# Latent attention's query projection: rotary columns taken once, and rotated for four heads together on VectorE

## The chip, the cores and the metric

One core of one Trainium2 chip runs the whole program. The time is device microseconds of one execution; the median of the runs is what is compared. In the text PE is TensorE (PEld its weight loads), DVE is VectorE, ACT is ScalarE, POOL is GpSimd and SP is the engine that issues the DMAs.

## What is computed

Two decoder layers on 256 tokens of width 1024, in float32. Each layer has parallel attention groups (eight heads of latent attention, eight heads of sparse attention), an output projection, cross-attention and a gated FFN. The change lies in the query side of the latent attention:

```python
def apply_rope(x, cos, sin):
    x1, x2 = jnp.split(x, 2, axis=-1)
    ...
    return jnp.concatenate([x1 * c - x2 * s, x1 * s + x2 * c], axis=-1)

def mla_mixer(cq, ckv, kr, cq_g, w_uq, ckv_g, w_ukv, cos, sin):
    q = (rms_norm(cq, cq_g) @ w_uq).reshape(B, S, MLA_HEADS, MLA_NOPE + MLA_ROPE)   # 8 heads x (64 + 32)
    kv = (rms_norm(ckv, ckv_g) @ w_ukv).reshape(B, S, MLA_HEADS, MLA_NOPE + MLA_V)
    q_nope = q[..., :MLA_NOPE]
    q_rope = apply_rope(q[..., MLA_NOPE:], cos, sin)
    k_nope, v = kv[..., :MLA_NOPE], kv[..., MLA_NOPE:]
    k_rope = apply_rope(kr[:, :, None, :], cos, sin)[:, :, 0]
    ...
        s = (jnp.einsum('bqhd,bkhd->bhqk', qn, k_nope)
             + jnp.einsum('bqhd,bkd->bhqk', qr, k_rope)).astype(jnp.float32) * scale
```

## The kernel before, in words

A float32 product is made of three matmuls on numbers split in two: `hi` is the rounded value and `lo` the rest, and hi x hi, lo x hi and hi x lo are added in PSUM. A piece of a weight is loaded by DMA into a `raw` buffer (four of them), ACT writes `hi` (L130), DVE writes `lo` = raw - hi (L131); `hi` and `lo` have six buffers each. The raw buffer is free for the next DMA when both have read it; a DMA that waits for one holds the queue of weights behind it, the pieces of the output projection `w_out` among them.

The attention of a layer is a list of steps, written in an order that is given for each layer (`mq0` to `mq3` are the calls of `mla_q` for two heads each, `mqk0` to `mqk3` those of `mla_qk`, `mkv` is `mla_kv`, `av` belongs to the sparse heads; the lists begin with the sparse heads' steps):

```
layer 0: ... ch qk3 kr mq2 mq0 fill mkv par2 mq1 mq3 av3 mqk2 mqk3 mqk0 mqk1 mav0 mav1 fill mav3 mav2
layer 1: ... ch qk3 kr mq0 mkv mq3 mq1 av3 mqk0 mq2 mqk1 mqk3 mav0 mav3 mqk2 mav1 mav2
```

A scheduler then orders the instructions of each engine by these steps, their dependences and its priorities. Each engine runs its list strictly in order. A PSUM tile is one bank: four for the tag `a` and four for the tag `b`; `mla` has `a`, the scores `mqk` have `b` in layer 0 and `a` in layer 1.

`mla_q` for two heads (`hp`) writes 256 columns of queries, 128 a head: 64 without rotation (nope), 32 for rotation, and these 32 once more with their halves swapped, made by two more splits of 128x96. Three tiles of the rank by three matmuls by two heads are 18 matmuls of 128x256 (L177 to L179). One DVE multiplication (L713) by a table with ones, cosines and sines moves both heads into `qT`. The scores (L721, L722) contract over 128 rows; on the key's side the rotated 32 rows stand twice, so the sum of the two products is the rotation. What follows for a head is a maximum on DVE (L545), an exponential on ACT (L548), a reciprocal and a product with it on DVE (L550, L154), transposes on PE (`pt`, L561) and their copy (`pT`, L564 on ACT or L566 on DVE; tag `pT`, four buffers), and the product with the values (`mpv`).

Of the kernel before, what the change touches and what calls it, by code (L numbers as in the profile page):

```python
# [10 lines left out]
F32 = mybir.dt.float32  # L11
# [42 lines left out]
def consts():  # L54
    f = np.float32
    ident = np.eye(P, dtype=f)
    q = np.arange(P)[:, None]
    k = np.arange(S)[None, :]
    dist = (P + q - k).astype(f)
    neg = np.where(dist >= 0, -dist, -BIG).astype(f)  # L60
    tri = np.where(dist >= 0, 0.0, -BIG).astype(f)
    inv = (np.float32(10000.0) ** (-np.arange(0, ROPE, 2, dtype=f) / np.float32(ROPE))).astype(f)
    ang = np.arange(S, dtype=f)[:, None] * inv[None, :]
    cos, sin = np.cos(ang).astype(f), np.sin(ang).astype(f)
    cs = np.ones((P, S), f)
    cs[64:80], cs[80:96] = cos.T, cos.T
    cs[96:112], cs[112:128] = -sin.T, sin.T
    kcs = np.concatenate([cos, cos, -sin, sin], 1).reshape(NT, P, 64).transpose(1, 0, 2)
    slopes = (2.0 ** (-8.0 * np.arange(1, HN + 1) / HN)).astype(f)
    t = np.arange(S).reshape(NT, P).T[:, :, None, None]  # L70
    cend = (np.arange(16) * 16 + 31)[None, None, None, :]
    ok = (cend <= t) & (np.arange(16) < NC)
    ok = np.broadcast_to(ok, (P, NT, HN, 16))
    ctab = np.where(ok, -(slopes * 8.0)[None, None, :, None] * (t - cend), -BIG).astype(f)
    return {
        "c_ident": ident, "c_neg": neg, "c_tri": tri, "c_cs": cs, "c_kcs": np.ascontiguousarray(kcs),
        "c_ctab": np.ascontiguousarray(ctab), "c_cok": np.ascontiguousarray(ok.astype(f)),
    }

# [10 lines left out]
def trunk(ctx: ExitStack, tc: tile.TileContext, a: dict, out: bass.AP):  # L90
# [41 lines left out]
        return hv, lv  # L132

    def wmat(w, cuts, ks=KD, cols=None, wn=None):
        """Column ranges of w [ks*128, :] split into (hi, lo), as a list over the rows' tiles."""
        n = sum(c1 - c0 for c0, c1 in cuts)
        per = max(1, 1024 // (wn or n))
        out_ = []
        for k0 in range(0, ks, per):
            k1 = min(ks, k0 + per)  # L140
            segs, o = [], 0
            for c0, c1 in cuts:
                segs.append(((0, k1 - k0), (o, o + c1 - c0),
                             w[k0 * P:k1 * P, c0:c1].rearrange("(k p) n -> p k n", p=P)))
                o += c1 - c0
            h, lo = piece(k1 - k0, n, segs, wn, cols)
            out_ += [(h[:, i], lo[:, i]) for i in range(k1 - k0)]
        return out_
# [15 lines left out]
        V.tensor_tensor(hl[1], x, hl[0].bitcast(F32), op=ALU.subtract)  # L164

    def mm_nat(o, xh_, xl_, t, ws):
        """o[token, col] += x @ w, x^T stationary."""
        for k, (h, lo) in enumerate(ws):
            T.matmul(o, xh_[:, t, k], h, start=k == 0, stop=False)  # L169
            T.matmul(o, xh_[:, t, k], lo, start=False, stop=False)  # L170
            T.matmul(o, xl_[:, t, k], h, start=False, stop=k == len(ws) - 1)  # L171

    def mm_tr(o, xh_, xl_, ws, m0):
        """o[col, token] += (x @ w)^T, w stationary."""
        ms = slice(m0, m0 + P)
        for k, (h, lo) in enumerate(ws):
            T.matmul(o, h[:, ms], xh_[:, :, k], start=k == 0, stop=False)  # L177
# [100 lines left out]
        return par[:, c:c + n]  # L278

    tri = const.tile([P, S], F32, name="c_tri", tag="c_tri")  # L280
    cs = const.tile([P, S], F32, name="c_cs", tag="c_cs")
    kcs = const.tile([P, NT, 64], F32, name="c_kcs", tag="c_kcs")
    ctab = const.tile([P, NT, HN, 16], F32, name="c_ctab", tag="c_ctab")
    cok = const.tile([P, NT, HN, 16], F32, name="c_cok", tag="c_cok")
# [79 lines left out]
    for l in range(DEPTH):  # L364
# [168 lines left out]
            V.tensor_tensor(ol[:, :, kt:kt + n], src, hi.bitcast(F32), op=ALU.subtract)  # L533

        def probs(heads, scale, shape, mult):
            """exp(scale * score + table - max) for each head; its rows' scales are left for norm()."""
            sm = st.tile(shape, F32, name="sm", tag="sm", bufs=8)
            out_ = []
            for parts, tables, sc, kind in heads:
# [150 lines left out]
        def mla_rope_k():  # L690
# [8 lines left out]
            else:  # L699
                for g in range(2):  # L700
                    V.tensor_copy(kT[g][64:128], pb[64:128, None, 0:S].to_broadcast([64, 4, S]))

        def mla_q(ch, hp):
            r2 = lambda v: v.rearrange("p k (h c) -> p (k h) c", h=2)
            cols = [(lambda v: r2(v), lambda v: r2(v)[:, :, 0:96]),
                    (lambda v: r2(v)[:, :, 80:96], lambda v: r2(v)[:, :, 96:112]),
                    (lambda v: r2(v)[:, :, 64:80], lambda v: r2(v)[:, :, 112:128])]
            ws = wmat(a["mla_w_uq"][l], [(hp * 192, (hp + 1) * 192)], ks=3, cols=cols, wn=256)
            pb = bank("mla")
            for i in range(2):  # L710
                mm_tr(pb[:, i * S:(i + 1) * S], ch[0], ch[1], ws, i * P)
            j = 2 * (hp % 2)
            V.tensor_tensor(qT[hp // 2][:, j:j + 2, :], pb.rearrange("p (i n) -> p i n", i=2),  # L713
                            cs[:, None, :].to_broadcast([P, 2, S]), op=ALU.mult)

        def mla_qk(hp):
            heads = []
# [61 lines left out]
        for name in cfg['attn'].split():  # L779
# [3 lines left out]
            if name in ("kr", "mq0", "mkv") and "qT" not in e:  # L783
                qT = e["qT"] = [big.tile([P, 4, S], F32, name=f"qT{g}", tag=f"q{g}") for g in range(2)]
                kT = [big.tile([P, 4, S], F32, name=f"kT{g}", tag=f"k{g}") for g in range(2)]
            steps[name]()

        gb = load_gb(a["ln1_g"][l], a["ln1_b"][l])
# [224 lines left out]
```

## Time and profile before

| | |
|---|---|
| median of three runs | 887.38 us (887.13, 887.38, 888.57) |
| profiled execution, span | 887.0 us |
| PE / PEld busy | 97% / 90% |
| DVE / ACT / POOL busy | 74% / 58% / 5% |
| chain that ended last | PE 88%, DVE 5%, DMA 3%, ACT 2% |

The profile is of one execution; its span stands 0.4 us under the median of the runs. Matmuls are pipelined, so the busy time of PE counts one matmul while the next has begun. The chain is followed back from the last instruction through what released each.

### The profile page before, as it was taken

The page shows a single profiled execution, that of the slowest core. Times are in us where ns is not written, and L with a number is a line of the kernel's source. Part 1 is how long each engine was busy: PE and PEld are TensorE (multiplying, and loading weights), DVE is VectorE, ACT ScalarE, POOL GpSimd, SP SyncE. Part 2 cuts the span into 40 slices and gives each one's busy share as a digit, 9 for nine tenths or more (in the row PEclk, how much of TensorE's full clock was granted, in tenths as well). Part 3 has the DMA queues.
Part 4 walks back from the last instruction along what each step waited for, and adds up shares of the span by engine and source line. Part 5 has one row for each costly group of instructions (what it writes and reads, how often), then busy time and mean ns, then how long its engine had stood idle before and what let it go on. Part 6 is the DMA issues. An engine that isn't in the chain of part 4 may idle for free.

```text
span 887.0 us, 15857 instructions
## 1 busy us (share of the span) xinstructions
PE 857.6 (97%) x6088; PEld 794.2 (90%) x6088; DVE 659.9 (74%) x1293; ACT 511.7 (58%) x938; POOL 44.8 (5%) x60
## 2 busy tenths in 40 slices
PE   3999999999999999999999999999999999999996
PEld 3989798899989999999989998879998899999995
DVE  6788887766587777677687788868566877767767
ACT  4669764545545565465555678636573476555551
POOL 1053100000000000000000020000000000000000
PEclk9999999999999999999999999999999999999998
DMA  8954463485247656556537734546633746656631
GB/s 243 301 154 122 130 188 99 144 260 166 95 143 238 190 178 208 184 167 206 176 119 199 216 90 109 143 131 212 192 116 110 236 149 205 200 161 188 214 122 48
DMA packets 128523, 149.76 MB, mean 169 GB/s; under 512 B 6289, under 2 KB 111039, under 8 KB 128447
## 3 DMA queue, kind: packets, MB, share of 16 engines
q1 hardware_dynamic: 128447, 148.75, 54.6%
q8 instruction: 48, 0.79, 0.4%
q14 instruction: 28, 0.23, 0.1%
HBM read 147.68 MB, written 1.05 MB: 168 GB/s over the span
## 4 chain that ended last, share of the span: by engine, by line
PE 88%; DVE 5%; DMA 3%; ACT 2%; issue 1%; SPq 0%; POOL 0%; DVEq 0%; ACTq 0%; POOLq 0%
PE up L179 9%; PE up L178 9%; PE up L177 9%; PE acc L947 4%; PE acc L948 4%; PE acc L949 4%; PE acc L170 3%; PE acc L169 3%; PE acc L171 3%; PE fill L171 2%; PE xq L179 2%; PE xq L178 2%; PE xq L177 2%; PE fill L169 2%; PE fill L170 2%; PE pt L561 2%
## 5 line engine op out<-in xcount | busy, mean ns | idle before, releaser
L131 DVE TENSOR_TENSOR lo<-raw,hi 128x1024 fp32r<-128x1024 f32 (+5 forms) x296 | 320.6, 1096 | 82.9 <-ACT hi L130 78.3
L130 ACT ACTIVATE hi<-raw 128x1024 fp32r<-128x1024 f32 (+5 forms) x296 | 279.7, 957 | 152.7 <-PE acc L171 34.6
L179 PE MATMUL up<-xTh,lo 128*128 128x256 f32 x672 | 190.2, 283 | 0.0
L178 PE MATMUL up<-xTl,hi 128*128 128x256 f32 x672 | 190.2, 283 | 0.0
L177 PE MATMUL up<-xTh,hi 128*128 128x256 f32 x672 | 190.2, 283 | 0.0
L178 PEld LDWEIGHTS up<-xTl,hi 128*128 128x128 f32 x672 | 128.9, 192 | 0.7
L177 PEld LDWEIGHTS up<-xTh,hi 128*128 128x128 f32 x672 | 128.9, 192 | 0.7
L179 PEld LDWEIGHTS up<-xTh,lo 128*128 128x128 f32 x672 | 128.9, 192 | 0.0
L931 DVE SCALAR_TENSOR_TENSOR cv<-up,par,cv 128x255 f32<-128x255 f32 x88 | 42.1, 479 | 51.6 <-ACT cv L930 51.5
L930 ACT ACTIVATE cv<-up,par 128x256 f32<-128x256 f32 x88 | 49.0, 559 | 52.6 <-PE up L179 48.0
L948 PE MATMUL acc<-lo,frh 128*128 128x512 f32 x176 | 68.8, 391 | 0.0
L947 PE MATMUL acc<-hi,frh 128*128 128x512 f32 x176 | 68.7, 392 | 0.0
L949 PE MATMUL acc<-hi,frl 128*128 128x512 f32 x176 | 68.2, 389 | 0.0
L548 ACT ACTIVATE p<-p,nm 128x128 f32<-128x128 f32 (+1 forms) x96 | 42.8, 450 | 9.5 <-DVE nm L545 9.3
L199 POOL TENSOR_TENSOR mv<-mv,mhalf 128x1 f32<-128x1 f32 x16 | 14.7, 920 | 650.5 <-DVE mv L223 497.6
L932 DVE SCALAR_TENSOR_TENSOR cv<-up,par,cv 128x254 f32<-128x254 f32 x88 | 42.0, 479 | 1.4
L937 ACT ACTIVATE frh<-cv 128x256 fp32r<-128x256 f32 x44 | 18.3, 419 | 37.8 <-DVE cv L935 37.6
L949 PEld LDWEIGHTS acc<-hi,frl 128*128 128x128 f32 x176 | 33.0, 188 | 7.5 <-DVE frl L938 0.6
L947 PEld LDWEIGHTS acc<-hi,frh 128*128 128x128 f32 x176 | 33.1, 188 | 6.9 <-ACT frh L937 0.8
L177 PE MATMUL projt<-xTh,hi 128*128 128x256 f32 x128 | 37.2, 292 | 1.9 <-DVE c2l L462 1.6
L948 PEld LDWEIGHTS acc<-lo,frh 128*128 128x128 f32 x176 | 33.1, 188 | 6.0
L178 PE MATMUL projt<-xTl,hi 128*128 128x256 f32 x128 | 37.0, 289 | 0.5 <-DVE xTl L240 0.5
(257 smaller groups left out, 2027.6 us busy)
## 6 DMA issues: line engine op xcount, KB each, us to landing
raw<-in_ffn_w_up SPq DMA_DIRECT2D x88, 512.0 KB, 4.9
raw<-in_ffn_w_down SPq DMA_DIRECT2D x44, 512.0 KB, 4.3
raw<-in_xa_wkv SPq DMA_DIRECT2D x32, 512.0 KB, 4.3
raw<-in_xa_wq SPq DMA_DIRECT2D x16, 512.0 KB, 4.6
raw<-in_xa_wo SPq DMA_DIRECT2D x16, 512.0 KB, 4.1
raw<-in_w_in SPq DMA_DIRECT2D x24, 256.0 KB, 4.8
raw<-in_w_out SPq DMA_DIRECT2D x16, 256.0 KB, 5.4
raw<-in_w_out SPq DMA_DIRECT2D x8, 512.0 KB, 5.1
```

Of the source, the lines that this page charges most:

```text
L130: A.activation(h_, x_, AF.Copy)
L131: V.tensor_tensor(l_, x_, h_.bitcast(F32), op=ALU.subtract)
L169: T.matmul(o, xh_[:, t, k], h, start=k == 0, stop=False)
L170: T.matmul(o, xh_[:, t, k], lo, start=False, stop=False)
L171: T.matmul(o, xl_[:, t, k], h, start=False, stop=k == len(ws) - 1)
L177: T.matmul(o, h[:, ms], xh_[:, :, k], start=k == 0, stop=False)
L178: T.matmul(o, h[:, ms], xl_[:, :, k], start=False, stop=False)
L179: T.matmul(o, lo[:, ms], xh_[:, :, k], start=False, stop=k == len(ws) - 1)
L930: A.activation(c, u, AF.Identity, bias=pcol("cb", l, ft), scale=w_[2])
L947: T.matmul(o, fh[:, ts_], h[:, cs_], start=f == 0, stop=False)
L948: T.matmul(o, fh[:, ts_], lo[:, cs_], start=False, stop=False)
L949: T.matmul(o, fl[:, ts_], h[:, cs_], start=False, stop=f == NF - 1)
```

## The change: rotary columns once, four heads at a time

`mla_q` now splits the 64 nope columns of its two heads (128x384 in all) and their 32 rotary columns (128x192) apart. The rotary columns of two calls (a pair: hp 0 and 1, or 2 and 3) go into one pair of tiles, `rhi` and `rlo`, from the same buffers as `hi` and `lo`, held until the second call of the pair. Each call has nine matmuls for nope; the second call of a pair has nine more for the rotary rows of four heads, into the other half of its PSUM bank. So a pair has 27 matmuls instead of 36. ACT copies the nope rows of each head into `qT`. In the second call of a pair DVE rotates 128 rows: a shuffle that swaps the halves of each head's 32 rows, a product with the cosines, one with the sines, and a sum; then four copies of 32x256, two on DVE and two on ACT, put the heads' rows into rows 64 to 95 of `qT`. Rows 96 to 127 are set to zero by GpSimd once a layer. `rc` and `rs` are two buffers of the tag `pT`.

```diff
-    cs = const.tile([P, S], F32, name="c_cs", tag="c_cs")
+    cs = const.tile([P, 2, S], F32, name="c_cs", tag="c_cs")
...
+        rw = {}
+
         def mla_q(ch, hp):
-            r2 = lambda v: v.rearrange("p k (h c) -> p (k h) c", h=2)
-            cols = [(lambda v: r2(v), lambda v: r2(v)[:, :, 0:96]),
-                    (lambda v: r2(v)[:, :, 80:96], lambda v: r2(v)[:, :, 96:112]),
-                    (lambda v: r2(v)[:, :, 64:80], lambda v: r2(v)[:, :, 112:128])]
-            ws = wmat(a["mla_w_uq"][l], [(hp * 192, (hp + 1) * 192)], ks=3, cols=cols, wn=256)
+
+            g, i = divmod(hp, 2)
+            last = g in rw
+            if not last:
+                rw[g] = [wp.tile([P, 3, P], F32R, name="r" + s, tag=s, bufs=HL) for s in ("hi", "lo")]
+            rh, rl = rw[g]
+            r = wp.tile([P, 1024], F32, name="raw", tag="raw", bufs=RAW)
+            rv = r[:, :576].rearrange("p (k n) -> p k n", k=3)
+            nc.sync.dma_start(rv, a["mla_w_uq"][l][:, hp * 192:(hp + 1) * 192].rearrange("(k p) n -> p k n", p=P))
+            h, lo = [wp.tile([P, 3, P], F32R, name=s, tag=s, bufs=HL) for s in ("hi", "lo")]
+            heads = lambda v: v.rearrange("p k (h c) -> p k h c", h=2)
+            ms = slice(64 * i, 64 * i + 64)
+            for cut, dh, dl in ((slice(0, 64), h, lo), (slice(64, 96), rh[:, :, ms], rl[:, :, ms])):
+                src, dh, dl = heads(rv)[:, :, :, cut], heads(dh), heads(dl)
+                A.activation(dh, src, AF.Copy)
+                V.tensor_tensor(dl, src, dh.bitcast(F32), op=ALU.subtract)
             pb = bank("mla")
-            for i in range(2):
-                mm_tr(pb[:, i * S:(i + 1) * S], ch[0], ch[1], ws, i * P)
-            j = 2 * (hp % 2)
-            V.tensor_tensor(qT[hp // 2][:, j:j + 2, :], pb.rearrange("p (i n) -> p i n", i=2),
-                            cs[:, None, :].to_broadcast([P, 2, S]), op=ALU.mult)
+            mm_tr(pb[:, 0:S], ch[0], ch[1], [(h[:, k], lo[:, k]) for k in range(3)], 0)
+            if last:
+                mm_tr(pb[:, S:2 * S], ch[0], ch[1], [(rh[:, k], rl[:, k]) for k in range(3)], 0)
+            for j in range(2):
+                A.activation(qT[g][0:64, 2 * i + j, :], pb[64 * j:64 * j + 64, 0:S], AF.Copy)
+            if last:
+                del rw[g]
+                rc, rs = [tmp.tile([P, S], F32, name=n, tag="pT", bufs=4) for n in ("rc", "rs")]
+                V.stream_shuffle(rs, pb[:, S:2 * S], [(c + 16) % 32 for c in range(32)])
+                V.tensor_tensor(rc, pb[:, S:2 * S], cs[:, 0], op=ALU.mult)
+                V.tensor_tensor(rs, rs, cs[:, 1], op=ALU.mult)
+                V.tensor_tensor(rc, rc, rs, op=ALU.add)
+                for j in range(4):
+                    copy_(qT[g][64:96, j, :], rc[32 * j:32 * j + 32], j % 2)
...
                 kT = [big.tile([P, 4, S], F32, name=f"kT{g}", tag=f"k{g}") for g in range(2)]
+                for g in range(2):
+                    G.memset(qT[g][96:128], 0.0)
```

The line numbers of the kernel before stand two higher than those of the changed one up to this place (L721 of before is L741 afterwards, L154 is L152). The scheduler's order moves with the change. On PE in layer 1, from the end of mq1, before (`pv` with `vsl` and `vwn` belongs to `av3`):

```order
L561 MATMUL pt<-c_ident,p 128x128 x12
L570 MATMUL pv<-pT,vsl 64x256
L571 MATMUL pv<-pT,vsl 64x128
L570 MATMUL pv<-pT,vsl 64x256
L571 MATMUL pv<-pT,vsl 64x128
L570 MATMUL pv<-pT,vwn 64x256
L571 MATMUL pv<-pT,vwn 64x128
L570 MATMUL pv<-pT,vwn 64x256
L571 MATMUL pv<-pT,vwn 64x128
L654 MATMUL pv<-pct,vct 64x256 x2
L721 MATMUL mqk<-kT_6441,qT_6439 128x128
L722 MATMUL mqk<-kT_6441,qT_6439 128x256
```

and after the change, from the end of the pair's rotary matmuls:

```order
L177 MATMUL mla<-xTh,rlo 128x256
L559 MATMUL pt<-c_ident,p 128x128 x10
L568 MATMUL pv<-pT,vsl 64x256
L569 MATMUL pv<-pT,vsl 64x128
L568 MATMUL pv<-pT,vsl 64x256
L569 MATMUL pv<-pT,vsl 64x128
L741 MATMUL mqk<-kT_6445,qT_6443 128x128
L742 MATMUL mqk<-kT_6445,qT_6443 128x256
L741 MATMUL mqk<-kT_6445,qT_6443 128x128
L742 MATMUL mqk<-kT_6445,qT_6443 128x256
L568 MATMUL pv<-pT,vwn 64x256
L569 MATMUL pv<-pT,vwn 64x128
```

The first score matmuls of `mqk0` moved ahead of the second half of the `pv` matmuls. On ACT at the same place, before (`hi` of 128x1024 is a piece of `w_out`):

```order
L687 ACTIVATE vmla<-mlav 128x512
L130 ACTIVATE hi<-raw 128x1024 x2
L564 ACTIVATE pT<-pt 128x384 x4
L130 ACTIVATE hi<-raw 128x1024
L532 ACTIVATE oTh<-pv 128x2x128
L548 ACTIVATE p,sm<-p,nm 128x128
```

and after the change:

```order
L725 ACTIVATE qT_6444<-mla 64x256 x2
L128 ACTIVATE hi<-raw 128x1024
L725 ACTIVATE qT_6443<-mla 64x256 x2
L562 ACTIVATE pT<-pt 128x384 x2
L128 ACTIVATE hi<-raw 128x1024
L156 ACTIVATE qT_6443<-rc 32x256 x2
L562 ACTIVATE pT<-pt 128x384 x2
L128 ACTIVATE hi<-raw 128x1024
```

The nope copies into `qT` (L725) and the rotary ones (L156) stand between the splits of `w_out` now, the rotary ones behind the split at L128. On DVE in layer 1, around the end of mq2, before (ISA is the maximum, L545, of `mqk`):

```order
L550 RECIPROCAL sm<-sm 128x2
L154 TENSOR_SCALAR p<-p,sm 128x128
L154 TENSOR_SCALAR p<-p,sm 128x256
L713 TENSOR_TENSOR qT_6440<-mla,c_cs 128x512
L550 RECIPROCAL sm<-sm 128x2
L545 ISA p,nm<-mqk,c_tri 128x128
L545 ISA nm 128x1
L154 TENSOR_SCALAR p<-p,sm 128x128
L154 TENSOR_SCALAR p<-p,sm 128x256
```

and after the change:

```order
L543 ISA p,nm<-mqk,c_tri 128x128
L543 ISA nm 128x1
L543 ISA p,nm<-mqk,c_tri 128x256
L543 ISA nm 128x1
L729 STREAM_SHUFFLE rs<-mla 128x256
L730 TENSOR_TENSOR rc<-mla,c_cs 128x256
L731 TENSOR_TENSOR rs<-rs,c_cs 128x256
L548 RECIPROCAL sm<-sm 128x2
L543 ISA p,nm<-mqk,c_tri 128x128
L543 ISA nm 128x1
L732 TENSOR_TENSOR rc<-rc,rs 128x256
L152 TENSOR_SCALAR p<-p,sm 128x128
L158 COPY qT_6444<-rc 32x256 x2
```

In the place of one multiplication (L713) the shuffle and its followers stand between the softmax steps of other heads.

## Rows read from the trace of the kernel before

**Rows 1.** The page's first lines: busy microseconds, share of the span and instructions of each engine; the chain of work that ended last, by engine; and one group of matmuls (busy us, mean ns of one | idle before).

```profile
span 887.0 us, 15857 instructions
...
PE 857.6 (97%) x6088; PEld 794.2 (90%) x6088; DVE 659.9 (74%) x1293; ACT 511.7 (58%) x938; POOL 44.8 (5%) x60
...
PE 88%; DVE 5%; DMA 3%; ACT 2%; issue 1%; SPq 0%; POOL 0%; DVEq 0%; ACTq 0%; POOLq 0%
...
L177 PE MATMUL up<-xTh,hi 128*128 128x256 f32 x672 | 190.2, 283 | 0.0
```

**Rows 2.** Busy us of PE, PEld, DVE, ACT and POOL in stretches of 10 us (ahead of them their end and the sum of PE alone; instructions in brackets), then the granted TensorE clock (1.00 is 2.4 GHz), the share of the DMA engines and GB/s.

```profile
120.00:130.00 10.00, 10.00 (x80) 8.64 (x79) 7.95 (x14) 6.53 (x10) 0.00 (x0) 1.00 0.91 241
...
550.00:560.00 10.00, 10.00 (x75) 9.51 (x75) 9.88 (x27) 8.43 (x22) 0.00 (x0) 1.00 0.06 22
560.00:570.00 10.00, 10.00 (x82) 8.91 (x81) 8.01 (x23) 6.52 (x16) 0.00 (x0) 1.00 0.98 261
570.00:580.00 10.00, 10.00 (x66) 8.09 (x65) 9.18 (x48) 6.53 (x27) 0.00 (x0) 1.00 0.16 57
```

**Rows 3.** The waits of 100 to 131 us (layer 0): who waited at which line, for what; us in total, times, longest.

```profile
DVE qT L713 <- PE mla L179: 0.9, 2, 0.6
...
PEld mqk L721 <- issue: 0.6, 2, 0.4
```

**Rows 4.** PE's time line in the query projection of layer 0: start, duration, line, operation.

```profile
107.63 0.28 PE L178 MATMUL mla<-xTl,hi 128*128 128x256 f32 x1
107.75 0.28 PE L179 MATMUL mla<-xTh,lo 128*128 128x256 f32 x1
107.87 0.28 PE L177 MATMUL mla<-xTh,hi 128*128 128x256 f32 x1
```

**Rows 5.** DVE from 95 to 130 us, grouped by line and shape: names, shapes and count | busy us, mean ns of one | idle before, releaser.

```profile
L713 DVE TENSOR_TENSOR qT<-mla,c_cs 128x512 f32<-128x512 f32 x4 | 2.8, 690 | 1.0 <-PE mla L179 0.9
...
L131 DVE TENSOR_TENSOR lo<-raw,hi 128x576 fp32r<-128x576 f32 x2 | 1.5, 755 | 0.0
...
L131 DVE TENSOR_TENSOR lo<-raw,hi 128x96 fp32r<-128x96 f32 x4 | 0.8, 256 | 0.0
```

**Rows 6.** ACT in the same stretch and form.

```profile
L130 ACT ACTIVATE hi<-raw 128x1024 fp32r<-128x1024 f32 x6 | 6.4, 1062 | 3.8 <-PE fill L178 3.3 <-PE mla L178 0.4
L564 ACT ACTIVATE pT<-pt 128x384 f32<-128x384 f32 x8 | 3.7, 488 | 2.0 <-PE pt L561 1.9
...
L130 ACT ACTIVATE hi<-raw 128x576 fp32r<-128x576 f32 x2 | 1.3, 670 | 0.0
...
L130 ACT ACTIVATE hi<-raw 128x96 fp32r<-128x96 f32 x4 | 0.9, 267 | 0.0
L532 ACT ACTIVATE oTh<-pv 128x256 fp32r<-128x256 f32 x2 | 0.8, 388 | 2.3 <-PE pv L654 2.3
```

**Rows 7.** DVE operations of 128x256 elsewhere (70 to 80 us): L154 with one tensor operand, in SBUF, L616 with two, one of them in PSUM.

```profile
L154 DVE TENSOR_SCALAR p<-p,sm 128x256 f32<-128x256 f32 x4 | 1.4, 350 | 0.0
...
L616 DVE TENSOR_TENSOR sc<-cmps,c_ctab 128x256 f32<-128x256 f32 x1 | 0.4, 424 | 0.0
```

**Rows 8.** PE's time line at the end of the query projection of layer 0 (runs of one form are one row).

```profile
125.94 0.29 PE L179 MATMUL mla<-xTh,lo 128*128 128x256 f32 x1
126.07 1.47 PE L561 MATMUL pt<-c_ident,p 128*128 128x128 f32 x12
...
128.31 0.49 PE L721 MATMUL mqk<-kT,qT 128*128 128x128 f32 x2
```

**Rows 9.** PE's time line around the query projections of layer 1.

```profile
561.54 0.28 PE L179 MATMUL mla<-xTh,lo 128*128 128x256 f32 x1
561.66 1.47 PE L561 MATMUL pt<-c_ident,p 128*128 128x128 f32 x12
563.07 0.75 PE L570 MATMUL pv<-pT,vsl 128*64 128x256 f32 x4
...
563.77 0.60 PE L570 MATMUL pv<-pT,vwn 128*64 128x256 f32 x3
...
568.87 0.39 PE L721 MATMUL mqk<-kT,qT 128*128 128x128 f32 x2
...
571.49 0.82 PE L561 MATMUL pt<-c_ident,p 128*128 128x128 f32 x6
```

**Rows 10.** DVE's time line there.

```profile
554.74 0.69 DVE L160 COPY kT<-mla 64x512 f32<-64x512 f32 x1
...
557.79 2.35 DVE L131 TENSOR_TENSOR lo<-raw,hi 128x1024 fp32r<-128x1024 f32 x2
560.17 0.69 DVE L713 TENSOR_TENSOR qT<-mla,c_cs 128x512 f32<-128x512 f32 x1
```

**Rows 11.** ACT's time line there.

```profile
553.75 0.58 ACT L682 ACTIVATE kT<-mla 64x512 f32<-64x512 f32 x1
```

**Rows 12.** The DMA queue's time line: a w_out piece is issued.

```profile
540.13 0.38 SPq L122 DMA_DIRECT2D raw<-in_w_out  x1
```

**Rows 13.** DMA issues of w_out: KB each, median us from issue to landing; the one issued at 540.13 and the next of that size, at 547.60.

```profile
raw<-in_w_out SPq DMA_DIRECT2D x1, 512.0 KB, 5.8
...
raw<-in_w_out SPq DMA_DIRECT2D x1, 512.0 KB, 3.6
```

**Rows 14.** GpSimd's memsets, whole span, by line and shape.

```profile
L447 POOL MEMSET kk<- 64x512 f32 x4 | 2.1, 522 | 55.6 <-PE xpv L875 51.9 <-issue 1.7 <-DMA raw<-in_w_in 1.7
```

More of the change, by code (lines that the diff above doesn't have):

```diff
@@ L64, in consts @@
     cos, sin = np.cos(ang).astype(f), np.sin(ang).astype(f)
-    cs = np.ones((P, S), f)
-    cs[64:80], cs[80:96] = cos.T, cos.T
-    cs[96:112], cs[112:128] = -sin.T, sin.T
+    cs = np.stack([np.tile(np.concatenate([cos.T, cos.T]), (4, 1)), np.tile(np.concatenate([-sin.T, sin.T]), (4, 1))], 1)
     kcs = np.concatenate([cos, cos, -sin, sin], 1).reshape(NT, P, 64).transpose(1, 0, 2)
@@ L75, in consts @@
     return {
-        "c_ident": ident, "c_neg": neg, "c_tri": tri, "c_cs": cs, "c_kcs": np.ascontiguousarray(kcs),
+        "c_ident": ident, "c_neg": neg, "c_tri": tri, "c_cs": np.ascontiguousarray(cs), "c_kcs": np.ascontiguousarray(kcs),
         "c_ctab": np.ascontiguousarray(ctab), "c_cok": np.ascontiguousarray(ok.astype(f)),
```

## Prediction

> **What bounds the kernel now.** The page comes first [rows 1]: TensorE is busy for 97% of an 887.0 us span, its weight loads for 90%, and the chain that ended last lies 88% on PE; VectorE has 74%, ScalarE 58%. By this the time is PE's list of work, and a matmul less is time gained, as long as PE finds its next one ready.
>
> Then the stages that the change touches, one stretch in each layer (105 to 136 us and 549 to 575 us). In the table of stretches [rows 2] PE is busy for 10.00 of 10 us there, at a granted clock of 1.00. The margin beside it differs: DVE has 7.95 us of work in 120–130, but 9.88 in 550–560 and 9.18 in 570–580. In layer 1 VectorE is nearly a second bound.
>
> The waits [rows 3] name no engine for which PE stands at the score matmuls (mqk, L721): they show 0.6 us of "issue", time in which nothing that the profile shows was late. The DVE eviction that makes qT (L713) waits for PE, not the other way round. The queries are early today; the question is whether they stay so.
>
> What a projection matmul costs is not the 283 ns that the page gives one of 128x256 (L177 [rows 1]). In the query projection the starts are 0.12 us apart [rows 4]; they overlap, so one fewer is worth 0.12 us.
>
> **What is removed.** Per layer 72 query matmuls become 54, in the program 36 fewer: 36 x 0.12 = **-4.3 us**, 2.16 in each layer. In layer 0 the gain is complete by the last projection matmul, which starts at 125.94 [rows 8] and would start at 123.8. In layer 1 it is complete by the end of mq1 (last start 561.54 [rows 9], which becomes 559.4), since it is mq0 and mq3 that lose nine matmuls each; mq2 behind them still issues 18.
>
> **What it adds on VectorE and ScalarE.** Before, one mla_q costs DVE 0.75 + 2 x 0.255 + 0.69 = 1.95 us [rows 5] and ACT 0.67 + 2 x 0.27 = 1.2 us [rows 6], so 7.8 and 4.8 us in a layer. After, the splits are 128x384 and 128x192. On DVE the first lies between 0.42 (128x256, L616 [rows 7]) and 0.69 (128x512, L713 [rows 5]), and I take 0.55; the second between 0.255 and 0.42, and I take 0.35. On ACT I take 0.49, the time of its 128x384 copy (L564), and 0.35 for the other, between 0.27 and 0.39 [rows 6]. A pair of mla_q adds on DVE a shuffle, three 128x256 operations of 0.42 by L616 and two 32x256 copies. The trace has no shuffle. Its bounds are 0.35, the one-operand pass of that width (L154), and 0.69, what an operation of twice the width takes (L713); I take 0.42, since it reads PSUM as L616 does. A copy has the 0.35 of L154. Layer sum on DVE: 4 x 0.9 + 2 x (4 x 0.42 + 0.7) = 8.4 us, +0.6. ACT: 4 x (0.84 + 2 x 0.39) + 4 x 0.39 = 8.0 us, +3.2, with 0.39 from oTh, a 128x256 copy out of PSUM. Neither total sets the time; when each piece comes does.
>
> The Trainium skill, VectorE: DVE Perf Modes, in its perf-mode tier table, gives a shuffle of 2048 columns about 2400 ns in its only mode; by that 256 columns would be about 0.3 us by my estimate, and each chain below about 0.1 us shorter. No row here shows one.
>
> **What it adds on the path.** From the last projection matmul to a usable qT there is one operation of 0.69 us today. Afterwards there is a chain on DVE: shuffle, cosine product, sine product, sum, first copy, 4 x 0.42 + 0.35 = 2.0 us, the other head's copy beside it on ACT; and the shuffle also waits for the two ACT copies of the nope rows out of the same PSUM bank, up to 0.7 more where ACT is late.
>
> The like pair in the trace is kT's two evictions of one bank: ACT reads at 553.75 for 0.58 [rows 11], DVE at 554.74 [rows 10]. They don't overlap either, though DVE had other work between. The Trainium skill, Advanced Engine Details and Errata, under Bank Collisions, says that TensorE, VectorE and ScalarE cannot use one PSUM bank within a partition in the same cycle: a rule against this change, since nope and rope rows share a bank, and by it the 0.7 is due in every chain where ACT is not early. The row doesn't contradict it.
>
> *Layer 0.* PE has 12 transposes and four pv matmuls from 126.07 to the first score matmul at 128.31 [rows 8]. All this starts 2.16 earlier: transposes at 123.9, pv, after the 1.41 us that twelve take in layer 1 too [rows 9], at 125.3. The transposes' copies (pT) now stand behind hi splits of 1.06 us [rows 6] and the qT copies on ACT, so I put them at 126.05 and PE waits 0.8. Six fill matmuls stand ahead of mqk and cover a part of the rest; the chain of the second pair (shuffle behind a lo split of 1.2, half of the two in [rows 10], and a pT copy ahead of its copies) ends near 128.4, another 0.4; and mixing pv, fill and mqk adds some 0.2 of issue gaps. **+1.4 us**; bounds 0.5 (mostly covered) and 2.2 (all given back).
>
> *Layer 1, first pair.* PE has the transposes (1.41) and four pv matmuls (0.70) [rows 9] from 559.5 and reaches mqk0 at 561.6, because mqk0 now stands ahead of half of the pv matmuls. On DVE the two lo splits that end at 560.1 today [rows 10] end at about 560.6: one L713 of 0.69 is gone before them, two splits of 0.55 have come. The shuffle starts there, and the first copy ends at 562.6: a wait of 1.0. The second head's copy is ACT's, behind the hi split of a w_out piece. There are four raw buffers; mla_q's raw tile is now held until its late second split (about 558.1), so that the piece issued at 540.13 today [rows 12] can only be issued then. At 4.7 us to landing, the mean of two [rows 13], it is there at 562.8, the hi split ends at 563.9, the copy at 564.2, when PE has waited another 0.9. **+1.9 us**; bounds 0.6 and 3.2 (3.6 and 5.8 us to landing, and the chain by 0.4 earlier or later).
>
> *Layer 1, second pair.* mq2 ends at 568.9 [rows 9] - 2.16 + 1.9 = 568.6. Behind it come mqk1 (1.3, half of the 2.62 that two such steps take from 568.87) and six transposes (0.7), so PE reaches mqk3 at 570.6. On DVE the shuffle stands behind the maxima of mqk1's first head: it starts at 570.0, the products end at 571.3, the sum, behind a reciprocal and a maximum, at 572.0, the copies, with a softmax product between, at 572.8. **+2.2 us**; bounds 1.0 and 3.2. Nothing else is ready on PE, since the acc matmuls stand behind mqk3. Late next are the softmax steps of mqk3, for which DVE gains the same pause.
>
> Costed at nothing: the GpSimd memsets, four of 32x1024, by the row of half that width 0.5 to 1.0 us each [rows 14] on an engine that is 5% busy, early in the stage (if one came late, its time would be added to the chain); 128 KB more of table in the first microseconds; and some projections that change places upstream (±0.5).
>
> Sum: -4.3 + 1.4 + 1.9 + 2.2 = +1.2 us, on the span of 887.0 it is 888.2; the median of the runs stands 0.4 above that span, so **888.6**.
>
> **Rivals.** *The waits stay covered (faster).* If ACT and DVE come to their chains as the lower bounds say, the waits are 0.5 + 0.6 + 1.0 = 2.1 and the time 885.2. For it: DVE stood idle in layer 0 for 0.9 us ahead of L713 [rows 3], and the transposes and fills lie between. Against it: 9.88 of DVE in 550–560. It ends below 885.6 where the waits sum to under 2.5 us.
>
> *The late w_out piece holds ACT (slower).* At 5.8 us to landing ACT's hi split slides, and with it the rope copy and the exponentials behind it; the second pair's wait goes to its bound: 1.4 + 3.2 + 3.2 = 7.8 and 890.9. For it: DMA is at 0.98 in 560–570 already [rows 2], with the other w_out pieces behind this one. Against it: 0.06 in 550–560, so that the queues are empty when it is issued. It decides where the waits pass 6.1 us.
>
> *The matmuls weigh what the page's mean says:* 36 x 0.283 = 10.2 us, and 882.7 even with the waits of the forecast. The pace of 0.12 excludes nearly all of it.
>
> **The numbers.** A change under 0.2%, 1.8 us, can hardly be told from none here: faster is below 885.6, slower above 889.2. Waits of 3.2 to 7 us (886.3 to 890.1) are the forecast, at 0.40; under 3.2 us is the first rival at 0.32, of which 0.06 lies above 885.6; above 7 is the second at 0.26; the full weight has 0.02. So faster 0.28, and of the forecast 0.06 lies above 889.2: slower 0.32, same 0.40. The range, 884.2 to 892.0, goes 1 us beyond both rivals' prices; the likeliest alone has 886.3 to 890.1.
>
> **What would show it.** 36 mla matmuls fewer at a pace of 0.12; PE waiting at mqk in both layers for a copy out of rc, 0.5 to 2.5 us at a place; ACT's hi split waiting for w_out near 562; a shuffle of about 0.42. If PE shows no wait at mqk, the time is near 884 and the walk above is wrong; if the waits there are beyond 3 us, or acc waits behind it, the second rival has it.

## Result, and the profile after the change

| | before | after |
|---|---|---|
| median | 887.98 us (four runs, 887.13 to 889.52) | 892.85 us (four runs, 891.67 to 894.24) |
| profiled execution, span | 887.0 us | 889.9 us |

The ratio is 1.0056, with a 95% interval of 1.0042 to 1.0070: the change costs 4.9 us (3.7 to 6.2). The forecast was +1.2, and its range ended at 892.0. The page of after, its first lines, the chain and the matmul group:

```profile
span 889.9 us, 15838 instructions
...
PE 857.9 (96%) x6052; PEld 790.1 (89%) x6052; DVE 661.8 (74%) x1305; ACT 517.9 (58%) x954; POOL 45.0 (5%) x64
...
PE 86%; DVE 7%; DMA 2%; ACT 2%; issue 1%; POOL 0%; SPq 0%; DVEq 0%; ACTq 0%; POOLq 0%
...
L177 PE MATMUL up<-xTh,lo 128*128 128x256 f32 x672 | 190.2, 283 | 0.0
```

Beside [rows 1]: 36 matmuls are gone, PE's busy time is not (857.6, now 857.9), and two more hundredths of the chain lie on DVE. The stretches of [rows 2] after the change, with three stretches of 2 us more:

```profile
120.00:130.00 10.00, 8.60 (x65) 7.34 (x64) 9.21 (x19) 8.54 (x15) 0.00 (x0) 1.00 0.99 247
550.00:560.00 10.00, 10.00 (x73) 9.33 (x73) 9.47 (x26) 9.14 (x26) 0.80 (x1) 1.00 0.11 34
560.00:570.00 10.00, 9.45 (x69) 7.58 (x67) 9.15 (x32) 9.78 (x26) 0.00 (x0) 1.00 0.92 233
570.00:572.00 2.00, 0.10 (x1) 0.00 (x1) 1.94 (x10) 1.98 (x7) 0.00 (x0) 1.00 0.72 174
572.00:574.00 2.00, 1.97 (x8) 1.62 (x8) 1.85 (x10) 1.37 (x6) 0.00 (x0) 0.63 0.90 324
574.00:576.00 2.00, 2.00 (x7) 0.88 (x6) 1.89 (x10) 1.57 (x7) 0.00 (x0) 0.52 0.08 31
570.00:580.00 10.00, 8.07 (x35) 5.50 (x35) 7.14 (x35) 5.68 (x20) 0.00 (x0) 0.83 0.34 106
```

PE, at 10.00 of 10 before, has 8.60, 9.45 and 8.07 in three of them; in 570–572 it is all but still, and behind that its clock is granted at about half, the 1.2 GHz level. Its time line at the places where it stands still (start, duration, what; in brackets the idle time and its releaser), in order the sparse heads' stage, layer 0, layer 1:

```profile
94.75 0.55 PE L559 MATMUL pt<-c_ident,p 128*128 128x128 f32 x3
96.68 0.43 PE L568 MATMUL pv<-pT,vsl 128*64 128x256 f32 x1 [1.38 <-ACT pT L562]
...
123.48 1.47 PE L559 MATMUL pt<-c_ident,p 128*128 128x128 f32 x12
126.35 0.81 PE L568 MATMUL pv<-pT,vsl 128*64 128x256 f32 x3 [1.40 <-ACT pT L562]
...
129.23 0.49 PE L741 MATMUL mqk<-kT,qT 128*128 128x128 f32 x2
...
561.25 0.81 PE L568 MATMUL pv<-pT,vsl 128*64 128x256 f32 x3 [0.28 <-ACT pT L562]
...
562.77 0.46 PE L741 MATMUL mqk<-kT,qT 128*128 128x128 f32 x2 [0.27 <-DVE qT L158]
...
569.28 0.82 PE L559 MATMUL pt<-c_ident,p 128*128 128x128 f32 x6
572.03 0.46 PE L741 MATMUL mqk<-kT,qT 128*128 128x128 f32 x2 [1.93 <-DVE qT L158]
```

To place the difference, the program is cut at PE's own starts, so that each stage can be compared with the same stage of another kernel. The "first part" ends at the first score matmul of the sparse heads; "sparse" ends at the first `mla` matmul of layer 0, "projection" at its last one, "layer 0" at the first `lnt`, "between" at layer 1's first `mla`, "layer 1" at the next `lnt`. The "rest" ends at the start of the last matmul. In us, worked out from the starts of PE's rows (`e1` is after once more):

```
          first part  sparse  projection  layer 0  between  layer 1    rest
before         65.05   40.45       20.45    44.65   378.76    53.92  275.69
after          63.15   41.93       18.28    47.52   378.27    57.05  275.68
e1             63.45   41.87       18.28    47.53   378.28    55.47  275.70
```

The first part wanders between 63.2 and 65.7 us over all the profiles here, in kernels that do the same there; it happened to be 1.9 us longer in the profiled execution of before. From the first score matmul on, after stands 4.8 us behind before, and e1 3.2 us. The ten runs below have the same columns, and this sum lies within the interval of each timed difference, e9's at its very end.

### The profile page after: what moved, and what is told of

Read it like the earlier page. It is cut to its first block, busy times and chain, and to the rows that moved or that the text cites. A ratio compares the mean times of both kernels' runs of the same rounds, so it can differ in the third digit from the quotient of the medians.

```text
span 889.9 us, 15838 instructions
## 1 busy us (share of the span) xinstructions
PE 857.9 (96%) x6052; PEld 790.1 (89%) x6052; DVE 661.8 (74%) x1305; ACT 517.9 (58%) x954; POOL 45.0 (5%) x64
## 4 chain that ended last, share of the span: by engine, by line
PE 86%; DVE 7%; DMA 2%; ACT 2%; issue 1%; POOL 0%; SPq 0%; DVEq 0%; ACTq 0%; POOLq 0%
PE up L177 9%; PE up L176 9%; PE up L175 9%; PE acc L969 4%; PE acc L970 4%; PE acc L971 4%; PE acc L167 3%; PE acc L169 3%; PE acc L168 3%; DVE lo L129 2%; PE fill L169 2%; PE fill L167 2%; PE xq L177 2%; PE xq L175 2%; PE xq L176 2%; PE fill L168 2%
## 5 line engine op out<-in xcount | busy, mean ns | idle before, releaser
L129 DVE TENSOR_TENSOR lo<-raw,hi 128x1024 fp32r<-128x1024 f32 (+4 forms) x272 | 311.9, 1154 | 86.1 <-ACT hi L128 81.8
L128 ACT ACTIVATE hi<-raw 128x1024 fp32r<-128x1024 f32 (+4 forms) x272 | 270.6, 1003 | 152.8 <-PE acc L169 33.6
L546 ACT ACTIVATE p<-p,nm 128x128 f32<-128x128 f32 (+1 forms) x96 | 42.6, 445 | 6.8 <-DVE nm L543 6.6
```

The source lines that it names most:

```text
L128: A.activation(h_, x_, AF.Copy)
L129: V.tensor_tensor(l_, x_, h_.bitcast(F32), op=ALU.subtract)
```

## Experiments

Each is after with the edit shown, unless it says before. "From qk" is the sum of the stages behind the first part, against before.

**The changed kernel once more, on another chip.**

> The changed kernel once more, for a second profile beside a kernel before on the same chip. If its time is a property of the kernel: 4 to 6 us over the kernel before, PE standing about 1.9 us ahead of the scores of mqk3 in layer 1 near 572 us, and a granted clock of 0.5 to 0.65 in the 4 us behind that. If the low clock was an accident of one execution, the second profile shows 1.00 there, and the span is about 1.7 us shorter at the end of layer 1's attention than the first one's, counted from its beginning.

Measured: 892.1 against 888.56 us, ratio 1.0050 (1.0022 to 1.0077), from qk +3.2. One of the eight executions took 900.31 us, which widens the interval; the medians differ by 3.5 us. The pauses are the same, 1.93 at mqk3 too, but the clock stayed at 1.00 behind it: layer 1 takes 55.47 us instead of 57.05. The fall of the clock is thus worth 1.6 us of one execution, and the rest is there without it.

**The gain alone.** Before, with the second head's nine matmuls left out in the first call of each pair:

```diff
-            for i in range(2):
+            first = hp // 2 not in seen
+            seen.add(hp // 2)
+            for i in range(1 if first else 2):
...
+            src = pb[:, None, 0:S].to_broadcast([P, 2, S]) if first else pb.rearrange("p (i n) -> p i n", i=2)
```

> The kernel before with 36 query matmuls left out (in the first call of each pair the second head's nine; its query rows are a copy of the first head's). Splits, evictions and their order on DVE and ACT stay. If a projection matmul is worth its pace of 0.12 us: -4.3 us, ratio 0.9951. If another engine is the bound beside PE (DVE at 9.88 of 10 us in 550 to 560): half of it or less, ratio 0.998 to 1.000.

Measured: 882.6 us, ratio 0.9931 (0.9913 to 0.9949), which is -6.1 us (-7.7 to -4.5); from qk -5.0, the profiled projection 18.28 us, 2.17 shorter. The matmuls are worth their pace of 0.12, and where nothing is added, all of it arrives at the end. By stages the gain is uneven: layer 1 is 3.02 us shorter, but layer 0 is 1.36 longer than before, with no wait of PE in it. The stage between is 1.20 shorter, most of it from one wait of PE in layer 1's first steps, 1.6 us before and 0.5 in e2:

```profile
PE projt L177 <- DVE c2l L462: 1.6, 1, 1.6
...
PE projt L177 <- DVE c2l L462: 0.5, 1, 0.5
```

This wait is 0.4 to 0.6 us in every kernel with the matmuls gone and 1.6 in e8, which has them all: about 1.1 us that the prediction did not have.

**The rotation left out**: four copies straight from PSUM.

```diff
-                rc, rs = [tmp.tile([P, S], F32, name=n, tag="pT", bufs=4) for n in ("rc", "rs")]
-                V.stream_shuffle(...)
...
-                    copy_(qT[g][64:96, j, :], rc[32 * j:32 * j + 32], j % 2)
+                    copy_(qT[g][64:96, j, :], pb[32 * j:32 * j + 32, S:2 * S], j % 2)
```

> The changed kernel without the rotation: the rotary rows are copied from PSUM into qT as they are (no shuffle, products, sum). If the chain on DVE is what PE waits for: waits at mqk under 0.5 us, no low clock in layer 1, 3 to 5 us less than the changed kernel (ratio to before 0.999 to 1.002). If it is ACT (its 16 more copies, and the hi split that waits for w_out), little changes: 0 to 1 us less, ratio 1.004 to 1.006.

Measured: 888.47 us, ratio 1.0007 (0.9992 to 1.0021). Layer 0 takes 44.93 us (before 44.65, after 47.52): without the rotation, and the two buffers of the tag `pT` that it takes, the loss there is all but gone. But the sparse stage stays 1.0 longer than before and layer 1 2.3 longer, with a wait for a copy to pT, so the rotation is not the whole of it:

```profile
570.77 1.06 PE L568 MATMUL mpv<-pT,vmla 128*64 128x256 f32 x2 [1.50 <-DVE pT L564]
```

The granted clock fell behind this wait too (0.71 and 0.50 in 570–574), so up to 1.6 of the 2.3 us may be the clock's.

**The pause at mqk3 filled** with 18 transposes that nobody needs:

```diff
+                if l == 1 and hp == 3 and i == 0:
+                    for _ in range(18):
+                        T.transpose(b0[:, 384:512], ident, ident)
```

> The changed kernel with 18 more transposes of the identity (about 2.1 us of PE, results unused) between mqk1 and the six transposes ahead of mqk3 in layer 1, where PE stood idle. If the low clock behind the gap costs time of its own: the granted clock there is 1.00 and the time falls by about 1.7 us against the changed kernel in spite of more work (ratio to before about 1.003). If the clock costs nothing that matters: the same as the changed kernel or up to 1 us more (ratio 1.005 to 1.007).

Measured: 892.71 us, ratio 1.0052 (1.0034 to 1.0070). The clock is 1.00 in all of 560–580 and mqk waits 0.4 us in sum, yet layer 1 takes 57.44: the filler took as much as the clock would have cost. It gives no version that is better, and it doesn't tell how often the clock falls in unfilled executions.

**A shorter chain**: the sum goes straight into qT, as four additions of 32x256 on DVE, without copies.

```diff
-                V.tensor_tensor(rc, rc, rs, op=ALU.add)
...
-                    copy_(qT[g][64:96, j, :], rc[32 * j:32 * j + 32], j % 2)
+                    rows = slice(32 * j, 32 * j + 32)
+                    V.tensor_tensor(qT[g][64:96, j, :], rc[rows], rs[rows], op=ALU.add)
```

> The changed kernel, where the sum of the two products is written by four DVE operations of 32x256 straight into qT, so that the four copies (two of them on ACT) are gone. If the length of the chain behind the last projection matmul is what costs: the stretch from the last mla matmul of layer 0 to the first transpose of its LayerNorm (lnt) falls from 47.5 us by 1 to 1.5, and PE's wait ahead of mqk3 in layer 1 falls from 1.9 to about 1.3; in all 1.5 to 2.5 us under the changed kernel (ratio to before 1.002 to 1.004). If it is the splits and nope copies on ACT: both stretches stay within 0.4 us.

Measured: 895.19 us, ratio 1.0094 (1.0070 to 1.0118). DVE's row in layer 1:

```profile
571.89 1.73 DVE L734 TENSOR_TENSOR qT<-rc,rs 32x256 f32<-32x256 f32 x4
```

One of them takes 0.42 us: an addition on 32 partitions takes as long as one on 128 (0.42), so DVE has 1.73 us where it had one sum and two copies of 0.3, and ACT's share of the copies has come to the engine that is late. The pause at mqk3 grew from 1.93 to 2.30.

**The pairs completed earlier.** Only the order of steps is changed: the two calls of a pair stand together, and the other pair's scores stand between.

```diff
-layer 0: ... kr mq2 mq0 fill mkv par2 mq1 mq3 av3 mqk2 mqk3 mqk0 mqk1 mav0 mav1 fill mav3 mav2
+layer 0: ... kr mq0 mq1 fill mkv par2 mq2 mq3 av3 mqk0 mqk1 mqk2 mqk3 mav0 mav1 fill mav3 mav2
-layer 1: ... kr mq0 mkv mq3 mq1 av3 mqk0 mq2 mqk1 mqk3 mav0 mav3 mqk2 mav1 mav2
+layer 1: ... kr mq0 mq1 mkv mq3 mq2 av3 mqk0 mqk1 mqk3 mav0 mav3 mqk2 mav1 mav2
```

> The changed kernel with another order of steps: layer 0 kr mq0 mq1 fill mkv par2 mq2 mq3 av3 mqk0 mqk1 mqk2 mqk3, layer 1 kr mq0 mq1 mkv mq3 mq2 av3 mqk0 mqk1 mqk3, so that a pair's calls stand next to each other and each pair's rotation has other PE work behind it. In this order ACT's first rotary split stands behind the sparse heads' exponentials in layer 0, no longer among them. If lateness of the queries and that split are the loss: the stretch from the first projection to the first mla matmul falls from 87.7 to about 86, the wait ahead of mqk3 is under 0.5, 4 to 6 us under the changed kernel (ratio 0.998 to 1.001). If DVE and ACT are simply full in these stages, whatever the order: 0 to 2 us (ratio 1.003 to 1.005).

Measured: 887.69 us, ratio 1.0002 (0.9990 to 1.0014), from qk 0.0. By the timed differences this is 4.7 us under after, as the first of the two expectations has it. Layer 0 takes 45.17, and all but 0.5 us of the loss there is gone. Layer 1 still takes 55.80: no wait for qT is left, but PE now waits for pT, by its time line:

```profile
562.51 0.81 PE L568 MATMUL pv<-pT,vsl 128*64 128x256 f32 x3 [1.61 <-ACT pT L562]
...
566.54 0.81 PE L568 MATMUL pv<-pT,vwn 128*64 128x256 f32 x3 [0.62 <-ACT pT L562]
```

and ACT's at the same place:

```profile
560.88 1.06 ACT L128 ACTIVATE hi<-raw 128x1024 fp32r<-128x1024 f32 x1 [0.28 <-DMA raw<-in_w_out]
561.97 0.87 ACT L562 ACTIVATE pT<-pt 128x384 f32<-128x384 f32 x2
564.05 1.06 ACT L128 ACTIVATE hi<-raw 128x1024 fp32r<-128x1024 f32 x1 [1.22 <-DMA raw<-in_w_out]
```

Twice a split of `w_out` stands ahead of the copies to pT, and its piece is not there. In the first wait of PE, 1.61 us, the missing piece has a part of 0.28 and the split itself 1.06; for the second piece ACT waits 1.22 us. Both pieces were issued after 557, since their raw buffers were held. The mechanism of the second rival is real, then; this order brings it out.

**Both of the last two together** (e6's order, e5's additions).

> Both of these at once, the order with early pairs and the sums straight into qT. If each takes away its own part: 5 to 7 us under the changed kernel, ratio to before 0.996 to 0.999. If the order alone already hides the chain: the same as with the order alone, within 1 us.

Measured: 891.9 us, ratio 1.0045 (1.0030 to 1.0060); PE's longest wait is 2.26 us for pT. The additions on DVE cost as much with the better order (3.8 us over e6; e5 is 3.4 over after).

**The order alone**: before, with e6's step lists.

> The kernel before with the same new order of steps, to tell what the order is worth without the change. If the order matters only by hiding the rotation: the time of the kernel before within 1 us (ratio 0.999 to 1.001). If the order is better in itself: ratio under 0.998, and what the early pairs gained in the changed kernel is not the rotation's.

Measured: 887.86 us, ratio 1.0000 (0.9985 to 1.0016), every stage behind the first part within 0.06 us of before. So the order is worth nothing by itself; what it gives in e6 is a repair of what the change did.

**Two buffers for a pair instead of three**: the rotary columns stand beside the first call's nope columns, in one wider tile.

```diff
-            if not last:
-                rw[g] = [wp.tile([P, 3, P], F32R, name="r" + s, tag=s, bufs=HL) for s in ("hi", "lo")]
-            rh, rl = rw[g]
+            n_ = P if last else 2 * P
...
-            h, lo = [wp.tile([P, 3, P], F32R, name=s, tag=s, bufs=HL) for s in ("hi", "lo")]
+            ht, lt = [wp.tile([P, 3, n_], F32R, name=s, tag=s, bufs=HL) for s in ("hi", "lo")]
+            if not last:
+                rw[g] = ht[:, :, P:2 * P], lt[:, :, P:2 * P]
+            rh, rl = rw[g]
+            h, lo = ht[:, :, 0:P], lt[:, :, 0:P]
```

> The changed kernel, where the rotary columns of a pair share the buffer of the first call's nope columns (256 columns wide), so that a pair holds two hi and two lo buffers as before the change, not three. In its order the pieces of w_out stand ahead of others as in the kernel before, and ACT's rotary split comes behind the exponentials of the sparse heads. If held buffers (and through them late splits, late raw buffers and a late w_out piece on ACT) are a part of the loss: the stretch to the first mla matmul falls from 87.7 to about 86.5, layer 0's stretch behind its last mla matmul from 47.5 to 46.5 or less, w_out is issued near 540 in layer 1 as before; the wait ahead of mqk3 stays (1.5 to 2). In all 2 to 3 us under the changed kernel, ratio 1.001 to 1.003. If only the chain matters: within 1 us of the changed kernel.

Measured: 895.55 against 889.8 us, ratio 1.0059 (1.0040 to 1.0078). The pieces of `w_out` are issued at 540.06 and 546.80 again, as in [rows 12], and it doesn't help: in layer 1 PE waits 1.22 for pT, 0.89 and 1.82 for qT, and the clock falls to 0.50. The early piece removes one cause, the late queries remain. The sparse stage stays 1.59 longer than before, against the expectation.

**Two buffers and e6's order.**

> Two buffers a pair and the order with early pairs together; in this order ACT's copies of av3's transposes stand ahead of the w_out splits, and both pairs of layer 1 are rotated while PE has the sparse heads' transposes and pv. If chain and held buffers are the whole loss: no wait over 0.6 us at mqk or pv in layer 1, the stretch from the first mla matmul of layer 1 to lnt near 52.5 (53.9 before, less 2.2, and some issue gaps), layer 0's near 45, in all about 3 us under the kernel before (ratio 0.995 to 0.998). If DVE and ACT are full in layer 1 whatever the order: 54.5 or more there, ratio 0.999 to 1.001.

Measured: 884.99 us, ratio 0.9945 (0.9928 to 0.9961), 4.9 us less than before (6.4 to 3.5): faster than both kernels, and within its error the whole worth of the matmuls. From qk it is -4.1: projection -2.17, layer 1 51.77, 2.15 under before, and what is left nearly cancels (sparse +0.83, layer 0 +0.16, between -0.78). PE's time line in layer 1:

```profile
559.37 1.47 PE L559 MATMUL pt<-c_ident,p 128*128 128x128 f32 x12
561.32 0.81 PE L568 MATMUL pv<-pT,vsl 128*64 128x256 f32 x3 [0.48 <-ACT pT L562]
...
562.49 0.49 PE L743 MATMUL mqk<-kT,qT 128*128 128x128 f32 x2
```

and the DMA queue's, where a piece of `w_out` that after issues past 557 stands:

```profile
544.67 0.37 SPq L120 DMA_DIRECT2D raw<-in_w_out  x1
```

The 0.48 us is the only wait of PE for another engine in 545–590. On ACT no split stands among the copies any more:

```profile
560.77 0.87 ACT L562 ACTIVATE pT<-pt 128x384 f32<-128x384 f32 x2
562.28 0.87 ACT L562 ACTIVATE pT<-pt 128x384 f32<-128x384 f32 x2 [0.63 <-PE pv L569]
```

The stages of all the kernels, as differences from before in us, with the timed difference and its interval:

```
       sparse  projection  layer 0  between  layer 1  from qk   timed
after    1.48       -2.17     2.87    -0.49     3.13     4.80    4.9 ( 3.7 ..  6.2)
e1       1.42       -2.17     2.87    -0.49     1.55     3.20    4.4 ( 2.0 ..  6.8)
e2       0.00       -2.16     1.36    -1.20    -3.02    -5.03   -6.1 (-7.7 .. -4.5)
e3       1.03       -2.16     0.28    -0.23     2.34     1.25    0.6 (-0.7 ..  1.9)
e4       1.12       -2.16     2.99    -0.47     3.53     5.00    4.6 ( 3.0 ..  6.2)
e5       1.67       -2.17     2.44    -0.40     4.93     6.48    8.3 ( 6.2 .. 10.5)
e6       0.76       -2.14     0.52    -1.05     1.88     0.01    0.2 (-0.9 ..  1.2)
e7       0.78       -1.36     2.05    -1.04     4.31     4.80    4.0 ( 2.7 ..  5.3)
e8       0.01        0.00    -0.03     0.06    -0.06    -0.03    0.0 (-1.3 ..  1.4)
e9       1.59       -2.17     1.67    -0.05     5.86     6.93    5.2 ( 3.6 ..  6.9)
e10      0.83       -2.17     0.16    -0.78    -2.15    -4.09   -4.9 (-6.4 .. -3.5)
```

The clock fell in layer 1 of the profiled executions of after, e3, e5, e7 and e9, and not in those of the others; so layer 1 and "from qk" can be compared to the microsecond only within each of these two groups.

## Why the prediction fell short

The direction was not called: "same" had the largest chance, the time was to be 888.6, and the kernel is slower by 4.9, well beyond the 1.8 us that can be told. By the steps of the prediction:

**The price of a matmul was right.** -4.3 us by the pace of 0.12: the projection is 2.14 to 2.17 us shorter (forecast 2.16) in every kernel with the matmuls gone but e7, and e10 shows 2.15 in layer 1. The rival of 283 ns a matmul is out.

**The base.** 887.0 was taken as a usual execution, 0.4 under the median. Profiled executions here run 1.8 us longer than their span (891.67 for 889.9), so it will have been the longest of the three runs shown. This changes nothing in the sum, but a comparison of the two spans alone (+2.9) would hide 1.9 us.

**The reordering upstream, costed at nothing with ±0.5, is the step that failed outright: +1.4 us.** The sparse stage takes 40.45 or 40.46 us in all three kernels with the old `mla_q` (before, e2, e8), and 41.2 to 42.1 in all nine with the new one. PE's row at 96.68 waits 1.38 us, and a row at 92.86 waits 0.64 for a copy to pT where before has one such wait of 0.31. ACT's time line ahead of it (the exponentials at L546 belong to a sparse head):

```profile
93.16 0.36 ACT L718 ACTIVATE rhi<-raw 128x192 fp32r<-128x192 f32 x1 [0.36 <-DMA raw<-in_mla_w_uq]
93.43 0.49 ACT L546 ACTIVATE p<-p,nm 128x256 f32<-128x256 f32 x1
...
95.67 0.49 ACT L546 ACTIVATE p<-p,nm 128x256 f32<-128x256 f32 x1
96.07 0.19 ACT L546 ACTIVATION_READ_ACCUMULATOR p<-p,nm 128x1 f32 x1
96.16 0.84 ACT L562 ACTIVATE pT<-pt 128x384 f32<-128x384 f32 x2
```

The transposes end near 95.3, but ahead of their copies ACT has a split that waits for its weights, and six exponentials, until 96.16. Before, ACT made its copies at 94.32 and at 96.83 with four exponentials between, and PE's pv matmuls, from 95.34 on, waited for none:

```profile
94.32 0.87 ACT L564 ACTIVATE pT<-pt 128x384 f32<-128x384 f32 x2
95.08 0.40 ACT L548 ACTIVATE p<-p,nm 128x128 f32<-128x128 f32 x1
...
96.83 0.47 ACT L564 ACTIVATE pT<-pt 128x384 f32<-128x384 f32 x1
```

So the copies come late behind six exponentials. That the new split brings this order about is not borne out: in e6, e7, e9 and e10 no rotary split stands near, the six exponentials stand ahead of the copies all the same, and PE waits 0.63 to 1.14 us there, against 0.91 to 1.57 where the split stands. For e9:

```profile
98.54 0.43 PE L568 MATMUL pv<-pT,vsl 128*64 128x256 f32 x1 [1.14 <-ACT pT L562]
```

Why the scheduler gives all nine kernels with the new `mla_q` this order, and none of the three with the old one, is open. The prediction walked the stages from 105 us on; this place lies ten us ahead of them.

**Layer 0, +1.4 with bounds to 2.2, measured +2.9: the mechanism was right, the size was not.** The qT copies and hi splits do stand ahead of the pT copies:

```profile
123.07 1.06 ACT L128 ACTIVATE hi<-raw 128x1024 fp32r<-128x1024 f32 x1 [0.79 <-DVE rc L730]
124.16 0.38 ACT L725 ACTIVATE qT<-mla 64x256 f32<-64x256 f32 x1
124.54 0.84 ACT L156 ACTIVATE qT<-rc 32x256 f32<-32x256 f32 x2
125.41 0.38 ACT L725 ACTIVATE qT<-mla 64x256 f32<-64x256 f32 x1
125.81 0.87 ACT L562 ACTIVATE pT<-pt 128x384 f32<-128x384 f32 x2
```

PE waits 1.40 for them where the walk had 0.8: from the start of the transposes (123.48) to the first pv matmul (126.35) it takes 2.87 us, and the walk had 2.15 (123.9 to 126.05). The 0.4 at the second pair did not come: PE's row at 129.23 shows no wait. Too small was also the cost of the mixing, put at 0.2. In e1, from PE's starts, the 20 pv matmuls of this stage take 3.42 us instead of 2.23; most of them stand in runs of one to three of a shape, with fills and scores between, where before has runs of four. The 96 acc matmuls take 23.10 instead of 22.32, the 36 transposes, with the wait, 4.80 instead of 3.42; fills and scores give 0.55 back. That the mixing is the reason is argued, not tested. Nor does such a loss need the rotation: in e2, where PE waits for nothing, the pv matmuls take 2.81 and the acc matmuls 22.97, and the layer is 1.36 us longer. How much of the 2.9 is the new order of PE's list alone, no run separates.

**Layer 1, first pair, +1.9, measured 0.55** (0.27 for qT, and 0.28 for pT, which the walk did not have). DVE's chain came as walked, with the shuffle at 560.75 and the first copy at 562.34 (forecast 560.6, and the copy's end at 562.6):

```profile
560.75 0.45 DVE L729 STREAM_SHUFFLE rs<-mla 128x256 f32<-128x256 f32 x1
561.09 0.41 DVE L730 TENSOR_TENSOR rc<-mla,c_cs 128x256 f32<-128x256 f32 x1
561.42 0.42 DVE L731 TENSOR_TENSOR rs<-rs,c_cs 128x256 f32<-128x256 f32 x1
561.87 0.43 DVE L732 TENSOR_TENSOR rc<-rc,rs 128x256 f32<-128x256 f32 x1
562.34 0.60 DVE L158 COPY qT<-rc 32x256 f32<-32x256 f32 x2
```

In e6 the shuffle waited 0.55 us until ACT's nope copies out of the same bank had ended:

```profile
560.65 0.01 DVE L729 LOAD_MASK_SELECT rs<-mla  x1 [0.55 <-ACT qT L725]
```

The rule on Bank Collisions (the Trainium skill, Advanced Engine Details and Errata) fits this order. But the wait is for a semaphore that ACT's copies raise, so the order stands in the program, and no run here lets the two engines meet in a bank. PE reached mqk0 later than walked, at 562.5 instead of 561.6, and so waited less. The 0.9 for ACT's copy did not come, and the step that failed there is the landing: the late piece of `w_out` was issued at 557.94 in e1 (forecast 558.1) and landed after 3.6 us, not 4.7.

**Layer 1, second pair, +2.2, measured 1.93**: right, and for the reason given, with DVE's chain between the softmax steps. That the layer as a whole came out near the forecast, 1.55 above before in e1 (forecast -2.16 + 4.1 = +1.9), is luck: its waits sum to 2.5 us, not 4.1, and another 1.2 lies in gaps of under 0.3 us and in changes of shape, which the walk of this layer did not have. Not forecast was that the clock can fall behind such a pause, 1.6 us more in the profiled execution.

**The rivals.** The time went past the price of "late w_out holds ACT" (890.9), but not by it: ACT's split at 561.47 follows the copies ahead of it without a wait for its piece. The excess over the forecast is +1.4 upstream, +1.5 in layer 0, -0.5 between the layers (with the 1.1 us that the wait at projt gave back), -0.4 in layer 1 and up to 1.6 by the clock, 2.0 to 3.6 us; the timed excess is 3.7 with an error of 1.3.

**What the runs settle.** The matmuls are worth their pace (e2, e10). What eats it is queries and pT copies that come late, from two sides: a pair that is complete only just ahead of its scores, and a third set of buffers that holds back the splits, the raw buffers and the pieces of `w_out`. The new order of steps alone takes 4.7 us off the changed kernel and only reaches before (e6: +0.2 us); two buffers alone take nothing off (e9: +5.2 us); both together bring the whole gain (e10). With the two buffers ACT's order moves too: in e6 a split stands between the transposes and their copies, in e10 none does. No run tells whether this order or the earlier pieces are what counts. One rival was not run: `rc` and `rs` hold two of the four buffers of the tag `pT`. In after no shuffle and no copy to pT waits for a reader of such a buffer, in e9 and e10 one copy does, for 0.63 us. Open are also the cause of the upstream order, and how much of the median the clock takes.

## What to carry over

Price a removed matmul at its pace, then look for each product that its successor waits for, in the order of the engines that make it: where PE is busy for 97% of the span, a copy that comes later than before can turn into a wait. When steps that ran one by one are tied into pairs, move the pairs ahead of their use and look at which buffers the pairing holds; here each alone brought no gain over before. And compare executions from a mark in the program behind the first loads, not by their spans.

## What the runs showed of the hardware

- A shuffle of 128x256 out of PSUM takes 0.444 us, all four within 0.003; the estimate by the perf-mode tier table (the Trainium skill, VectorE: DVE Perf Modes), about 0.3 us, is too low here, and L616's 0.42 [rows 7] was the nearer row. The estimate went by the columns alone; by L616's 0.42 for 256 columns and L713's 0.69 for 512, about 0.16 us of a pass on DVE does not go with them (an estimate from these two rows).
- An addition on DVE takes 0.42 us for 32x256 (e5, all sixteen) and 0.42 for 128x256 (after): a quarter of the partitions saves nothing here.
- The same pause of 1.93 us at mqk3 was followed by a granted clock of 0.63 and 0.52 in one execution (after) and of 1.00 in the other (e1). Pauses of 1.50 (e3), 2.30 (e5) and 2.26 us (e7) in layer 1 were followed by a fall, one of 1.61 (e6) was not: here the length of a pause alone does not tell. Before had such a fall too, in the first part of its profiled execution, behind a pause of 1.73 us:

```profile
52.35 0.43 PE L487 MATMUL cmp<-c_ident,hs 34*128 34x34 f32 x4 [1.73 <-DVE hs L160]
...
52.00:54.00 2.00, 1.65 (x9) 1.61 (x10) 2.00 (x4) 1.84 (x4) 2.00 (x2) 0.68 0.70 190
54.00:56.00 2.00, 2.00 (x11) 2.00 (x10) 2.00 (x12) 0.14 (x2) 1.88 (x3) 0.50 0.83 253
56.00:58.00 2.00, 2.00 (x17) 2.00 (x17) 1.02 (x4) 1.84 (x6) 1.21 (x2) 0.96 0.60 209
```
